# The DMAs of the output-weight sums, pinned to their place in the source's order

## The chip, the cores and the metric

The kernel runs on one core of one Trainium2 chip. The metric is device time in microseconds (us). The engines are called PE (TensorE, matrix products), DVE (VectorE), ACT (ScalarE), POOL (GpSimd) and SP (SyncE, which here does nothing but issue DMAs). Each engine works through its own list of instructions strictly in order; an instruction that waits for a semaphore holds up everything behind it on that engine.

## What is computed

The reference is one layer of a streaming encoder on 528 positions (512 inputs and 16 learned ones) of width 2048, batch 1:

```
u = rms_norm(h);  proj = u @ w_in              # 11600 columns: all inputs of both branches
A: score = sum_h w[t,h] * relu(iq[t,h] . ik[s]);  top 128 keys per query
   attention of 8 heads over these keys in a 256-wide latent space, with a bias by distance
B: softmax(q1 k1 + bias) - lam * softmax(q2 k2 + bias), 8 heads, chunk-causal; norm per head
mix = sigmoid(g_a) * ((o_a * silu(z_a)) @ w_o_a) + sigmoid(g_b) * ((o_b * silu(z_b)) @ w_o_b)
return h + rms_norm(mix @ w_out)               # w_out: 2048 x 2048
```

## The kernel before

Every product is computed with its operands split into a high and a low part, three matmuls in place of one (`mm3`, lines 288 to 291). The stages follow one another:

- **The first columns and the normalised input**, to about 90 us.
- **The index stage**, 90 to 250 us. The 16 index heads come in eight tiles of two. Tiles 2 to 7 each take two weight tiles of 512 KB ("halves"): SP loads one into `raw` (line 152), ACT makes its high part (156), DVE its low part (158), PE multiplies (289 to 291). Then PE makes the scores of the two heads (549, 550), ACT takes the relu (570), and DVE adds them up in `sc` (575).
- **Branch B**, eight heads, 230 to about 660 us. A head projects three *units* (`qb`, `kb`, `vb`). Per unit SP loads two halves of weights (187); ACT finds each half's sum of squares (`squares`, 123); POOL takes the largest over the partitions (128); DVE makes a power-of-two scale (`power_of_two`, 135 to 140); ACT and DVE split (169, 170); PE multiplies 48 or 96 times. The attention of a head runs between the products of the next one. Raw weights have room for three units, split weights for two. DVE also does the top-k search here (620, 624), a few rounds per half unit.
- **Branch A** (eight heads), the gates, the two branch projections, and from 1440 us **the output product**. This one is computed in Strassen's way: seven products in place of eight, on sums of the quarters of `w_out`. Those sums are what this case is about.

`wt_chain(k, n, tags)` makes four sums of quarters for one 128 x 512 piece, with DMAs alone: it loads two pieces (264, 265), adds another piece of DRAM to each in flight (263, a DMA issued by POOL that accumulates), stores both (260, by SP), and then twice more adds to the second tile and stores it. So one chain is load, add, put, add, put, add, put, each waiting for the one before. There are 16 chains, 32 loads, 64 adds and 64 puts, each of 256 KB; all write to DRAM (`tscr`), and the first reader of it is the output product. In the source a head of branch B starts two chains, and each of the six calls of `between()` in that head takes every chain one step on; the last step falls into the next head's first call. Chains of even and odd heads use different tiles.

The order in which instructions stand on an engine is not the source's. A scheduler of the framework puts each instruction at the place at which, by its own reckoning, it can first start; what has no operand from the computation, such as loads of weights, moves far ahead. `tc.keep_in_program_order(ins)` gives it one more edge: `ins` is queued behind the instruction that the source issued last on the same engine. It is an order of issue alone, with no wait for that instruction to finish. An instruction without such an edge may still move ahead of pinned ones.

Of the kernel before, what the change touches and what calls it, by code (L numbers as in the profile page):

```python
# [16 lines left out]
ALU = mybir.AluOpType  # L17
# [51 lines left out]
def layer_kernel(ctx, tc, xt_d, xn_d, cols_d, w0_d, wi_d, wkv_d, wo_d, wout_d, lam_d, post_d,  # L69
                 oh_d, rb_d, out_d):  # L70
    nc = tc.nc
# [8 lines left out]
    tscr = [nc.dram_tensor(f"wout_t{i + 1}", [8, P, 1024], F32, kind="Internal").ap() for i in range(4)]  # L80
# [173 lines left out]
    def wt_chain(k, n, tags):  # L254

        t = [opool.tile(HB, F32, tag=tag, name="wt") for tag in tags]
        q = [[wout_d[ci, di, k, :, 512 * n:512 * n + 512] for di in range(2)] for ci in range(2)]

        def put(i, x):
            nc.sync.dma_start(tscr[i][k, :, 512 * n:512 * n + 512], x)  # L260

        def add(x, src):
            nc.gpsimd.dma_start(x, src, accum_op=ALU.add)
        nc.sync.dma_start(t[0], q[0][0])
        nc.sync.dma_start(t[1], q[0][1])
        yield
        add(t[0], q[0][1])
        add(t[1], q[1][1])
        yield
        put(0, t[0])  # L270
        put(2, t[1])
        yield
        add(t[1], q[0][0])
        yield
        put(1, t[1])
        yield
        add(t[1], q[1][0])
        yield
        put(3, t[1])
# [488 lines left out]
    def qstack(acc, un, h):  # L768

        q = stack64(acc, un, ap_, "q", 4)  # L770
        for m in range(2):
            hs = slice(64 * m, 64 * m + 64)
            nc.scalar.activation(QZ[h % 2][m][hs], acc[hs], AF.Copy, scale=un[hs])
        return list(q) + QZ[h % 2]
# [107 lines left out]
    for h in range(NH):  # L882
        for i in range(2):
            wt_now.append(wt_chain(h, i, [f"o{6 + 4 * (h % 2) + 2 * i + x}" for x in range(2)]))
        for acc, un in proj_q("qb", h):
            step(2 if len(pending) == 7 else 1)
            between()
        q = qstack(acc, un, h)
        for acc, un in proj_kv("kb", h):
            step()  # L890
            between()
        kk = kstack(acc, un)
        if h == NH - 1:
            small_weights(0)
        for acc, un in proj_kv("vb", h):
            step()
            between()
        vt = ap_.tile([P, T], F32, tag="vt", name="vt", bufs=1)
        for t in range(2):
            nc.scalar.activation(vt[:, t * TH:(t + 1) * TH], acc[t][:, :TH], AF.Copy, scale=un)  # L900
        step(len(pending))
        pending = b_attend(h, q, kk, vt)
# [259 lines left out]
    for i in list(range(NDIRECT, NH, 2)) + list(range(NH, 2 * NH, 2)):  # L1162
        def end(x, d, i=i):
            gate_o(i + x, d.o[x], d.r[x])
        n, c0 = ("za", i) if i < NH else ("zb", i - NH)
# [335 lines left out]
```

## Time and profile before

| | |
|---|---|
| time, median of 3 (range) | 1601.42 us (1599.41 to 1604.9) |
| profiled execution | 1604.09 us, its span 1602.1 us |
| busy share of the span | PE 90%, DVE 69%, ACT 61%, POOL 9% |
| TensorE clock granted, mean | 0.961 of full speed |
| moved by DMA | 257.27 MB, 161 GB/s on average |

The profile is one execution. Busy shares are averages over stages; an idle engine is shown with the time that it sat idle and with what ended the wait. Durations of single instructions, the landing times of DMAs and the share of time in which the core's 16 DMA engines were busy come from the same execution.

### The profile page before, as it was taken

The page shows a single profiled execution, that of the slowest core. Times are in us where ns is not written, and L with a number is a line of the kernel's source. Part 1 is how long each engine was busy: PE and PEld are TensorE (multiplying, and loading weights), DVE is VectorE, ACT ScalarE, POOL GpSimd, SP SyncE. Part 2 cuts the span into 40 slices and gives each one's busy share as a digit, 9 for nine tenths or more (in the row PEclk, how much of TensorE's full clock was granted, in tenths as well). Part 3 has the DMA queues.
Part 4 walks back from the last instruction along what each step waited for, and adds up shares of the span by engine and source line. Part 5 has one row for each costly group of instructions (what it writes and reads, how often), then busy time and mean ns, then how long its engine had stood idle before and what let it go on. Part 6 is the DMA issues. An engine that isn't in the chain of part 4 may idle for free. (4 is left out here: it accounts for less than half of the span.)

```text
span 1602.1 us, 25286 instructions
## 1 busy us (share of the span) xinstructions
PE 1435.1 (90%) x9475; PEld 1076.2 (67%) x9475; DVE 1103.8 (69%) x2091; ACT 977.2 (61%) x1735; POOL 144.8 (9%) x199
## 2 busy tenths in 40 slices
PE   7895665689999999999999999999999899999997
PEld 7674443467666776656658888888888544448885
DVE  7963244376677766777567888877778555666788
ACT  6352243376666666777668778777777644436555
POOL 3512324100000000000000000000000011100001
PEclk9898777799999999999999999999999999999999
DMA  6499999932333323333264544444444544547674
GB/s 208 144 303 271 253 262 263 252 93 83 97 100 88 97 81 87 113 120 99 67 198 157 185 160 141 149 140 132 132 133 145 197 149 155 155 124 260 227 248 155
DMA packets 104218, 257.27 MB, mean 161 GB/s; under 512 B 12072, under 2 KB 16392, under 8 KB 103968
## 3 DMA queue, kind: packets, MB, share of 16 engines
q1 hardware_dynamic: 86224, 223.86, 43.4%
q0 software_dynamic: 9216, 16.78, 6.1%
q10 hardware_dynamic: 8656, 15.02, 2.6%
q8 instruction: 74, 1.21, 0.3%
q14 instruction: 48, 0.39, 0.1%
HBM read 211.42 MB, written 47.41 MB: 162 GB/s over the span
## 5 line engine op out<-in xcount | busy, mean ns | idle before, releaser
L123 ACT ACTIVATE junk<-raw 128x1024 bf16<-128x1024 f32 x192 | 201.9, 1052 | 168.0 <-DMA raw<-in_wi_dram 147.5
L289 PE MATMUL acc<-u,hi 128*128 128x264 f16 (+1 forms) x832 | 266.5, 320 | 17.5 <-ACT hi L169 16.8
L1015 PEld LDWEIGHTS <-wh 128*128 128x128 f16 x2464 | 241.6, 98 | 59.9 <-issue 31.4
L291 PE MATMUL acc<-u,lo 128*128 128x264 f16 (+1 forms) x832 | 266.1, 320 | 1.0 <-DVE lo L170 1.0
L290 PE MATMUL acc<-u,hi 128*128 128x264 f16 (+1 forms) x832 | 266.3, 320 | 0.0
L1015 PE MATMUL acc<-tu,wh 128*128 128x256 f16 x1408 | 235.6, 274 | 26.9 <-DVE r L1024 16.3
L169 ACT ACTIVATE hi<-raw,scale 128x1024 f16<-128x1024 f32 x104 | 118.9, 1145 | 131.4 <-PE acc L290 130.2
L1015 PE MATMUL acc<-tu,wl 128*128 128x256 f16 x704 | 192.7, 274 | 0.0
L1015 PE MATMUL acc<-u,wh 128*128 128x256 f16 x1056 | 175.3, 273 | 0.0
L289 PEld LDWEIGHTS <-hi 128*128 128x128 f16 x1088 | 107.6, 99 | 97.2 <-ACT hi L169 17.1
L170 DVE SCALAR_TENSOR_TENSOR lo<-raw,scale,hi 128x1024 f16<-128x1024 f32 x104 | 132.7, 1279 | 56.7 <-ACT hi L169 56.5
L291 PEld LDWEIGHTS <-lo 128*128 128x128 f16 x1088 | 107.5, 99 | 78.1 <-DVE lo L170 1.5
L290 PEld LDWEIGHTS <-hi 128*128 128x128 f16 x1088 | 107.6, 99 | 73.1 <-issue 1.2
L170 DVE SCALAR_TENSOR_TENSOR wl<-S,scale,wh 128x1024 f16<-128x1024 f32 x88 | 112.8, 1282 | 55.9 <-ACT wh L169 55.8
L1015 PE MATMUL acc<-u,wl 128*128 128x256 f16 x528 | 143.9, 273 | 0.0
L128 POOL PARTITION_ALL_REDUCE rows<-ssq x90 | 43.9, 488 | 1085.8 <-ACT junk L123 1029.3
L1015 PEld LDWEIGHTS <-wl 128*128 128x128 f16 x1232 | 120.8, 98 | 14.4
L169 ACT ACTIVATE wh<-S,scale 128x1024 f16<-128x1024 f32 x88 | 100.3, 1141 | 30.1 <-DVE S L1126 30.1
L158 DVE TENSOR_TENSOR lo<-raw,hi 128x1024 fp32r<-128x1024 f32 x40 | 48.8, 1223 | 73.9 <-ACT hi L156 73.5
L289 PE MATMUL acc<-og,hi 128*128 128x512 f16 x256 | 97.0, 379 | 0.0
L291 PE MATMUL acc<-og,lo 128*128 128x512 f16 x256 | 97.0, 379 | 0.0
L290 PE MATMUL acc<-og,hi 128*128 128x512 f16 x256 | 97.0, 379 | 0.0
(313 smaller groups left out, 2944.3 us busy)
## 6 DMA issues: line engine op xcount, KB each, us to landing
raw<-in_wi_dram SPq DMA_DIRECT2D x172, 512.0 KB, 4.9
wt<-in_wout_dram POOLq DMA_DIRECT2D x64, 256.0 KB, 7.6
wout_t<-wt SPq DMA_DIRECT2D x64, 256.0 KB, 5.9
raw<-in_wo_dram SPq DMA_DIRECT2D x32, 512.0 KB, 6.0
raw<-wout_t SPq DMA_DIRECT2D x32, 512.0 KB, 3.8
raw<-in_wout_dram SPq DMA_DIRECT2D x24, 512.0 KB, 3.6
wt<-in_wout_dram SPq DMA_DIRECT2D x32, 256.0 KB, 4.8
sg<-r ACTq DMA_DIRECT2D x32, 256.0 KB, 2.7
```

What stands on the lines that cost most here:

```text
L123: nc.scalar.activation(j, src, AF.Square, accum_out=dst)
L128: nc.gpsimd.partition_all_reduce(r, ssq, P, bass_isa.ReduceOp.max)
L158: nc.vector.tensor_sub(lo, raw, f32(hi))
L169: nc.scalar.activation(hi, src, AF.Copy, scale=s)
L170: nc.vector.scalar_tensor_tensor(lo, src, s, hi, op0=ALU.mult, op1=ALU.subtract)
L289: nc.tensor.matmul(out, aH, bH, start=start, stop=False)
L290: nc.tensor.matmul(out, aH, bL, start=False, stop=False)
L291: nc.tensor.matmul(out, aL, bH, start=False, stop=stop)
L1015: nc.tensor.matmul(acc, a[:, k, :], b, start=first and k == 0 and x == 0, stop=last and x == 2, skip_group_check=True)
```

## The change

The loads, the adds and the puts of `wt_chain` get the edge of `keep_in_program_order`. Nothing is added or removed: the same DMAs with the same operands.

```diff
         def put(i, x):
-            nc.sync.dma_start(tscr[i][k, :, 512 * n:512 * n + 512], x)
+            tc.keep_in_program_order(nc.sync.dma_start(tscr[i][k, :, 512 * n:512 * n + 512], x))

         def add(x, src):
-            nc.gpsimd.dma_start(x, src, accum_op=ALU.add)
-        nc.sync.dma_start(t[0], q[0][0])
-        nc.sync.dma_start(t[1], q[0][1])
+            tc.keep_in_program_order(nc.gpsimd.dma_start(x, src, accum_op=ALU.add))
+        for i in range(2):
+            tc.keep_in_program_order(nc.sync.dma_start(t[i], q[0][i]))
         yield
```

What this does to the lists, first on SP in the second half of the index stage. `raw_1528` and `raw_1530` are the two halves of the first unit of branch B; `wt` are tiles of the chains, with four numbers per head. Before:

```order
L260 DMA wout_t1<-wt_2855 128x512
L187 DMA raw_1528<-in_wi_dram 128x1024
L260 DMA wout_t4<-wt_2324 128x512
L260 DMA wout_t4<-wt_2328 128x512
L260 DMA wout_t3<-wt_2856 128x512
L260 DMA wout_t2<-wt_2852 128x512
L264 DMA wt_3382<-in_wout_dram 128x512
L265 DMA wt_3383<-in_wout_dram 128x512
L264 DMA wt_3386<-in_wout_dram 128x512
L187 DMA raw_1530<-in_wi_dram 128x1024
L260 DMA wout_t2<-wt_2856 128x512
L260 DMA wout_t4<-wt_2852 128x512
```

and now:

```order
L152 DMA raw_1407<-in_wi_dram 128x1024
L152 DMA raw_1467<-in_wi_dram 128x1024
L187 DMA raw_1528<-in_wi_dram 128x1024
L187 DMA raw_1530<-in_wi_dram 128x1024
L187 DMA raw_1539<-in_wi_dram 128x1024
L187 DMA raw_1541<-in_wi_dram 128x1024
L152 DMA raw_1570<-in_wi_dram 128x1024
L187 DMA raw_1798<-in_wi_dram 128x1024
L187 DMA raw_1845<-in_wi_dram 128x1024
L187 DMA raw_1847<-in_wi_dram 128x1024
L265 DMA wt_1873<-in_wout_dram 128x512
L265 DMA wt_1874<-in_wout_dram 128x512
```

All chain DMAs have left the index stage; the first chain (`wt_1873`) starts behind the loads of the first units of branch B. Next, SP in a head of branch B, with one put pair and the next head's loads; before, only the rows of lines 187, 656, 749 and 756 stood here:

```order
L656 DMA G_3832<-bias_rows 128x528
L187 DMA raw_3322<-in_wi_dram 128x1024
L187 DMA raw_3324<-in_wi_dram 128x1024
L260 DMA wout_t4<-wt_2852 128x512
L260 DMA wout_t4<-wt_2856 128x512
L265 DMA wt_3382<-in_wout_dram 128x512
L265 DMA wt_3383<-in_wout_dram 128x512
L265 DMA wt_3386<-in_wout_dram 128x512
L265 DMA wt_3387<-in_wout_dram 128x512
L187 DMA raw_3467<-in_wi_dram 128x1024
L749 DMA o9_f32<-ob_3283 128x512
L187 DMA raw_3469<-in_wi_dram 128x1024
```

Eight puts and four loads now stand between the six loads of raw weights of a head. Last, POOL in the first two heads; a `rows` is the largest sum of squares of one unit. Before:

```order
L128 ISA rows_2339<-ssq_2112 128x2
L128 ISA rows_2492<-ssq_2262 128x2
L263 DMA wt_5496<-in_wout_dram 128x512
L263 DMA wt_5500<-in_wout_dram 128x512
L128 ISA rows_2689<-ssq_2409 128x2
L128 ISA rows_2869<-ssq_2597 128x2
L128 ISA rows_3022<-ssq_2790 128x2
```

and now:

```order
L128 ISA rows_2339<-ssq_2112 128x2
L128 ISA rows_2492<-ssq_2262 128x2
L263 DMA wt_2323<-in_wout_dram 128x512
L263 DMA wt_2324<-in_wout_dram 128x512
L263 DMA wt_2327<-in_wout_dram 128x512
L263 DMA wt_2328<-in_wout_dram 128x512
L263 DMA wt_2324<-in_wout_dram 128x512
L263 DMA wt_2328<-in_wout_dram 128x512
L128 ISA rows_2689<-ssq_2409 128x2
L263 DMA wt_2324<-in_wout_dram 128x512
L128 ISA rows_2869<-ssq_2597 128x2
L263 DMA wt_2328<-in_wout_dram 128x512
```

Here six adds, which wait for loads and puts of their chain, stand ahead of the maximum `rows_2689`; from the next head on a round of eight adds lies between three maxima.

## Rows read from the trace of the kernel before

**Rows 1.** Stretches: length, busy us (instructions) per engine, clock, DMA share, GB/s.
```profile
120.00:140.00 20.00, 20.00 (x97) 16.26 (x96) 12.36 (x19) 8.70 (x19) 4.92 (x6) 1.00 1.04 305
140.00:160.00 20.00, 1.83 (x11) 1.31 (x9) 0.00 (x0) 0.00 (x0) 6.45 (x8) 0.62 1.00 238
160.00:180.00 20.00, 8.60 (x33) 6.93 (x33) 3.19 (x5) 4.78 (x10) 6.09 (x7) 0.70 0.95 250
...
300.00:320.00 20.00, 10.43 (x43) 5.77 (x44) 5.69 (x15) 7.75 (x14) 2.11 (x3) 0.61 0.83 238
sum 180.00, PE 101.03 PEld 72.89 DVE 62.72 ACT 57.40 POOL 51.75; mean PE 11.23 PEld 8.10 DVE 6.97 ACT 6.38 POOL 5.75
```
**Rows 2.** Timeline of PE: start, length, line; the wait before it and who ended it.
```profile
168.45 0.59 PE L549 MATMUL lg<-ikh,q 128*128 128x264 f32 x1 [26.61 <-ACT relu L570]
...
205.94 0.59 PE L549 MATMUL lg<-ikh,q 128*128 128x264 f32 x1 [8.80 <-ACT relu L570]
...
221.87 0.79 PE L289 MATMUL acc<-xh,hi 128*128 128x512 f32 x1 [7.76 <-ACT hi L156]
...
276.19 0.40 PE L289 MATMUL acc<-u,hi 128*128 128x264 f16 x1 [16.80 <-ACT hi L169]
...
310.05 0.90 PE L716 MATMUL acc<-ident,vt 128*128 128x128 f32 x3 [7.53 <-ACT vt L900]
```
**Rows 3.** Timeline of SP's queue, 155 to 171 us.
```profile
155.30 3.72 SPq L260 DMA_DIRECT2D wout_t<-wt  x4
159.11 1.11 SPq L187 DMA_DIRECT2D raw<-in_wi_dram  x1
...
170.93 0.38 SPq L187 DMA_DIRECT2D raw<-in_wi_dram  x1
```
**Rows 4.** Timeline of ACT, the load's first reader.
```profile
165.84 1.06 ACT L123 ACTIVATE junk<-raw 128x1024 bf16<-128x1024 f32 x1 [29.16 <-DMA raw<-in_wi_dram]
```
**Rows 5.** Timeline of POOL, a maximum behind adds.
```profile
193.10 0.37 POOL L128 PARTITION_ALL_REDUCE rows<-ssq  x1 [6.95 <-DMA wt<-in_wout_dram]
```
**Rows 6.** One whole head of branch B, columns as in rows 1.
```profile
399.60:442.20 42.60, 40.42 (x296) 29.97 (x295) 29.91 (x84) 28.33 (x56) 1.06 (x3) 1.00 0.31 94
```
**Rows 7.** Line 263's durations (ns); then landings of lines 263, 260, 265, 187.
```profile
L263 POOL DMA_DIRECT2D wt<-in_wout_dram x64: 853/862/2252, 78.8 to 309.6; - x64
...
DMA to landing us min/median/max: 3.9/7.6/12.8
...
DMA to landing us min/median/max: 2.0/5.9/8.2
...
DMA to landing us min/median/max: 3.1/6.0/6.7
...
DMA to landing us min/median/max: 3.7/4.5/9.1
```
**Rows 8.** DMA queues: packets, MB, packet time as share of 16 engines' span.
```profile
q1 hardware_dynamic: 86224, 223.86, 43.4%
q0 software_dynamic: 9216, 16.78, 6.1%
```
**Rows 9.** Timelines of SP, ACT, POOL, DVE and ACT in a head.
```profile
414.90 3.19 SPq L187 DMA_DIRECT2D raw<-in_wi_dram  x2
...
421.70 1.06 ACT L123 ACTIVATE junk<-raw 128x1024 bf16<-128x1024 f32 x1 [1.91 <-DMA raw<-in_wi_dram]
...
422.94 0.35 POOL L128 PARTITION_ALL_REDUCE rows<-ssq  x1 [15.50 <-ACT junk L123]
...
423.33 0.15 DVE L135 TENSOR_REDUCE exp<-rows 128x1 f32<-128x2 f32 x1 [5.60 <-POOL rows L128]
...
424.73 1.15 ACT L169 ACTIVATE hi<-raw,scale 128x1024 f16<-128x1024 f32 x1
```
**Rows 10.** Waits by pair, 330 to 660 us; then SP's queue, whole run: us, times, longest.
```profile
ACT hi L169 <- PE acc L290: 33.2, 15, 4.1
...
SPq L187 <- DVE lo L170: 204.2, 41, 15.4
```

## The prediction

> **What bounds the kernel now.** I read the busy time in stretches of 20 us first, from the start. The reader is to see a stage that falls out of the pattern: from 120 to 140 us PE is busy for all of the stretch, and a whole head of branch B keeps it busy for 40.42 of 42.6 us, so PE sets the pace there [rows 1, 6]; but in the nine stretches from 140 to 320 us it works 101.0 of 180 us, and its clock is granted at 0.61 to 0.70 in five of them [rows 1]. In the same stretches the DMA engines are busy for 0.83 to 1.0 and more of the time, against 0.31 in a head later on [rows 1, 6]. So some 79 us of PE's time are lost in the second half of the index stage and in head 0.
>
> Next I read who ended PE's waits there. Eight waits make up the 79 us; the largest are 26.61, 8.80, 7.76, 16.80 and 7.53 us, each ended by an ACT instruction [rows 2]. ACT itself waited: before 165.84 us it stood 29.16 us idle, at the sum of squares of a half that had not landed [rows 4]. In SP's queue that half was issued at 159.11, behind four puts that began at 155.30, and the next half only at 170.93, behind four more [rows 3]. The puts wait for adds. So the chain is: add still under way, put blocks SP, raw weights are issued late, ACT stands at the late half, relu and split stand behind it, PE stands. The weights need no such wait by themselves. POOL shows the same once more: the maximum at 193.10 had waited 6.95 us behind an add for a load of a chain [rows 5].
>
> **What the change takes away.** By the order of SP all 160 chain DMAs leave the index stage, and the loads of the first units stand together, ahead of the first chain. First term: the 79.0 us of idle PE. Second term, the clock: 33 matmuls took 8.60 us at a clock of 0.70, 97 took 20.00 us at full clock, so 33 would take 6.8: 1.8 us lost [rows 1]. Five stretches have such a clock, the others little or no loss; I take 8 us in all, between 0 and busy time times missing clock over the nine stretches, 17. Together 87 us.
>
> **What stays of it.** The last half of the index weights takes the place of the first unit's first half, so its load waits for that split; before, such a load cost PE the wait of 7.76 us [rows 2]. An undisturbed load lands 3.7 us after issue, not 8 [rows 7], so about 4 us stay. A similar wait at the start of branch B (third unit, whose second half is loaded into space that only the end of the index stage frees) gets 4 us. Bounds 0 and 15; I take 8.
>
> **What the change adds: the chains in branch B.** Work first. The 64 adds moved 16.78 MB in 6.1% of 16 engines' span, 98 us; other DMAs took 43.4% for 223.86 MB, 3.1 us per MB, so the 25.2 MB of chain loads and puts 78 us [rows 8]. Per head that is 22 us on top of 0.31 x 42.6 = 13 [rows 6]: a share of 0.83, below 1. Bandwidth alone does not stop a head.
>
> Then the waits. One round of a head's chains is a load, three adds and two puts, each waiting for the one before; the put that ends it stands on SP ahead of the next head's loads. By shortest landings that is 3.1 + 3 x 3.9 + 2 x 2.0 = 18.8 us, by medians 6.0 + 3 x 7.6 + 2 x 5.9 = 40.6, by the longest 6.7 + 3 x 12.8 + 2 x 8.2 = 61.5 [rows 7]; four adds in a row at 0.86 and four DMAs on SP make about 4 us more. The medians are those of a stage at a DMA share of 1. A head at 0.83 lies three quarters of the way from 0.31 to 1.0, so I go three quarters of the way from shortest to median: load 5.3, add 6.7, put 4.9, a round of 5.3 + 20.1 + 9.8 + 4 = 39 us. A head lasts 42.6 [rows 6]. The round fits, with 3 us to spare.
>
> Who is queued behind these waits? On SP, the raw loads. In a head a load is issued when DVE has split the old contents (SP waits for that, 41 times in the run [rows 10]), lands 4 us later, and then sum of squares, maximum and scale follow at once: 421.70, 422.94, 423.33; the next split on ACT begins at 424.73, behind them [rows 9]. What makes room in that is the split itself: ACT starts it as soon as PE frees a buffer, and waits for PE 15 times [rows 10], while PE needs it a unit later, 14.2 us (a third of a head). Both halves take 2.3 us on ACT, so some 11 us of delay cost nothing. On POOL, the maxima: in a steady head one of three stands behind three adds, the first two of which need a put landed and the third two more links. From the first add of the round: four adds issued and landed 10.2, put 4.9, two adds 8.4, put 5.2, one add 0.9: 30 us, against two units, 28.4. It comes 1 to 2 us late, inside the 11. So a steady head pays nothing as long as the round fits. I take 2 us over heads 2 to 7; bounds 0 and, if each pays 4, 24.
>
> The start is worse. In head 1 six adds stand between the maxima `rows_2492` and `rows_2689`, and in DVE's list the scale from the second one stands ahead of the low part of an earlier unit, which PE needs. From the first add of head 0 to there: 10.2 + 4.9 + 8.4 + 4.9 + 8.4, put and loads 6.6, then 10.2 + 4.9 + 1.7 + 0.4 = 61 us. In that time PE has the rest of `kb` of head 0, then `vb`, `qb`, `kb` at 11.1 us each and part of an attention, about 47. PE waits 14 us; with the shortest landings the way is 41 us and it waits 0, with medians about 20. I take 10, since the DMA engines have not yet reached 0.83 there.
>
> **Sum.** 79 + 8 - 8 - 2 - 10 = 67 us of the profiled execution's 1604.1, so 1537. That execution lay 2.7 us above the median of 1601.4, which gives 1534.
>
> **A rule that speaks against it.** An add holds POOL for 0.86 us in the median, but one took 2.25 [rows 7]; DVE was busy for 62.7 of 180 us beside them, and is for 29.9 of 42.6 in a head [rows 1, 6]. If DVE's work is what makes an add slow to issue, adds in branch B take longer: 1.4 us more each, for seven adds in the round 10 us, a round of 49 and 6 us more per head: 1534 + 7 x 6 = 1576. The Trainium skill, page "SBUF — State Buffer", section "SBUF: two separate sides", has such a rule: while DVE runs certain instructions that take both ports, GpSimd cannot write the descriptors of its DMAs. The trace hardly bears that out here: the median is 9 ns above the minimum. This rival gets 0.05.
>
> **Rivals.**
> - *The heads take on the wait* (0.18). At median landings the round is 45 us, over 42.6; with late raw loads 46 is near. For it: SP, a list in order, now carries waits for adds between raw loads, the same pattern that stopped PE before. Against it: landings outside the crowded stage are shorter. 7 x 3.4 = 24 us: 1558.
> - *The waits are gone without a price* (0.12). Shortest landings: the hitch in head 1 and the rest vanish, 87 us less: 1514; with shorter waits before 140 us, down to 1508.
> - *The index stage meets another limit* (0.05). If room for raw weights, not SP's order, holds the loads (rows 10 show that wait in its longest form, 15.4 us), PE waits as before: 1601. Against it: from 120 to 140 us loads came in time and PE was full.
> - *Slower* (0.07). Adds in branch B land as late as the longest seen, 12.8: a round of 45 + 3 x 5.2 = 61, PE waits 18 us in each of seven heads, 126 in place of the 2: 1658. It decides from a round of about 52 us on, where seven heads lose the 67 us. Against it: DMA share 0.83.
>
> **Numbers.** The forecast has 0.53 and a range of its own from 1518 to 1552. All cases: 1508 with everything gone; at the other end own waits 15, start 20 and 24 for the heads leave 87 - 59 = 28, so 1573, and the rule's 1576 is near. Range 1508 to 1576; what lies outside is the slower case and no change. About 5 us (0.3%) is what a measurement of this kernel can tell from nothing: faster 0.53 + 0.18 + 0.12 + 0.05 = 0.88, same 0.05, slower 0.07.
>
> **What would show it.** In the profile after: PE busy over 18 of 20 us in stretches from 140 us to the end of the index stage, which comes at about 195 and not 250; a DMA share near 0.3 there and near 0.8 in branch B; no wait of ACT over 10 us for raw weights in the index stage; one wait of PE of 5 to 15 us in head 1, behind `rows_2689`; stores of head results 42 to 44 us apart. I am wrong if these lie 46 us or more apart, or if PE still waits over 20 us in the index stage.

## The result and the profile after

The changed kernel took 1554.01 us in the median of its runs (1552.04 to 1558.84), the kernel before 1603.16 beside it (1599.41 to 1606.07): a ratio of 0.970, with a 95% interval of 0.967 to 0.973. The forecast was 1534 with a range of 1508 to 1576. So the direction and the range held, and 20 us of the forecast gain did not come. The main case's own range, 1518 to 1552, was missed by 2 us.

The stretches of the profile after, with the columns of [rows 1]: length, busy us (instructions) of PE, PEld, DVE, ACT and POOL, clock, DMA share, GB/s. The fifth row is one head, from one store of a head result to the next, and answers to [rows 6].

```profile
140.00:160.00 20.00, 19.87 (x94) 15.82 (x93) 11.34 (x20) 10.09 (x22) 0.38 (x1) 1.00 0.26 79
160.00:180.00 20.00, 19.92 (x98) 14.87 (x97) 12.74 (x21) 13.49 (x26) 3.96 (x12) 1.00 0.32 88
180.00:200.00 20.00, 20.00 (x131) 13.63 (x130) 18.70 (x56) 12.89 (x27) 3.09 (x6) 1.00 0.64 208
...
220.00:240.00 20.00, 12.23 (x60) 6.94 (x59) 5.83 (x17) 8.23 (x14) 4.64 (x7) 0.83 0.86 237
372.07:421.82 49.75, 43.11 (x296) 31.91 (x295) 32.17 (x90) 28.43 (x56) 8.68 (x12) 0.90 0.74 188
```

From 140 to 200 us PE is full at full clock, where before it worked 1.83 of 20 us at worst. That loss is gone, and the last scores of the index stage come at 188.2 us and not at 243.1. But the head lasts 49.75 us and not 42.60, with the same 296 matmuls.

The stores of head results date the rest. These are four of them in SP's queue (start, length, line), the first, the third, the fourth and the seventh:

```profile
281.79 0.96 SPq L749 DMA_DIRECT2D o_f<-ob  x1
...
372.07 0.33 SPq L749 DMA_DIRECT2D o_f<-ob  x1
421.82 0.33 SPq L749 DMA_DIRECT2D o_f<-ob  x1
...
566.29 0.32 SPq L749 DMA_DIRECT2D o_f<-ob  x1
```

Before, the first was issued at 357.16 and the seventh at 617.16. So 75.4 us are gained up to the first store. The six heads after it take 284.5 us in place of 260.0 (47.4 each in place of 43.3; the head shown is the second longest of them) and give 24.5 back, and what follows gives back another 3: 48 us of span, from 1602.1 to 1554.1.

How much of the 24.5 us is idle time, and how much a lower clock? The six heads, before and now:

```profile
357.16:617.16 260.00, 245.72 (x1767) 181.72 (x1766) 183.75 (x500) 169.52 (x331) 6.38 (x18) 0.99 0.31 92
```
```profile
281.79:566.29 284.50, 254.00 (x1766) 188.56 (x1765) 185.70 (x501) 170.10 (x331) 44.49 (x62) 0.94 0.74 192
```

For the same matmuls PE is busy 8.3 us longer, at a granted clock of 0.94 in place of 0.99, and idle for 16.2 us more.

Who waits in these six heads? Waits by pair (us in all, times, longest) of ACT, PE and DVE, before (357 to 617 us) and now (282 to 567 us):

```profile
ACT junk L123 <- DMA raw<-in_wi_dram: 31.7, 25, 4.3
...
PE acc L675 <- DVE pr L744: 11.0, 6, 2.2
...
DVE kl L785 <- ACT kh L784: 2.5, 6, 0.4
```

```profile
ACT junk L123 <- DMA raw<-in_wi_dram: 63.5, 24, 5.7
...
PE acc L675 <- DVE pr L744: 28.8, 6, 6.6
...
DVE kl L785 <- ACT kh L784: 41.3, 6, 7.5
DVE z L742 <- ACT p L668: 27.9, 8, 4.7
DVE exp L135 <- POOL rows L128: 7.8, 14, 1.6
```

PE has one long wait in each head, at the transposes of the softmax result `pr`. The chain behind it can be read in one head, on SP, ACT, DVE and PE:

```profile
371.51 0.33 SPq L187 DMA_DIRECT2D raw<-in_wi_dram  x1
...
373.80 0.33 SPq L187 DMA_DIRECT2D raw<-in_wi_dram  x1
...
379.44 1.06 ACT L123 ACTIVATE junk<-raw 128x1024 bf16<-128x1024 f32 x1 [4.77 <-DMA raw<-in_wi_dram]
...
380.49 0.51 ACT L668 ACTIVATE pr<-pr,mx 128x272 f32<-128x272 f32 x1
...
383.69 1.06 ACT L123 ACTIVATE junk<-raw 128x1024 bf16<-128x1024 f32 x1 [2.09 <-DMA raw<-in_wi_dram]
...
395.44 1.06 ACT L123 ACTIVATE junk<-raw 128x1024 bf16<-128x1024 f32 x1 [1.39 <-DMA raw<-in_wi_dram]
...
398.89 1.06 ACT L123 ACTIVATE junk<-raw 128x1024 bf16<-128x1024 f32 x1 [2.30 <-DMA raw<-in_wi_dram]
...
400.07 0.47 ACT L784 ACTIVATE kh<-acc,scale 64x264 fp32r<-64x264 f32 x1
...
381.63 0.16 DVE L742 RECIPROCAL z<-z 128x1 f32<-128x1 f32 x1 [4.08 <-ACT p L668]
...
400.58 0.48 DVE L785 SCALAR_TENSOR_TENSOR kl<-acc,scale,kh 64x264 fp32r<-64x264 f32 x1 [6.62 <-ACT kh L784]
...
408.90 1.94 PE L675 MATMUL acc<-ident,pr 128*128 128x128 f32 x8 [6.58 <-DVE pr L744]
```

The halves issued at 371.51 and 373.80 are first read at 379.44 and 383.69, 8 and 10 us later; in [rows 9] the second half, issued at about 418, was read at 421.70, 4 us later. ACT works through its list in order. Its sum of squares (line 123) stands idle for the half, the exponentials of the softmax (line 668) stand right behind it in the list, and DVE waits 4.08 us for them; PE still has work then. The same thing happens with the next two halves, and now it reaches PE. Their sums of squares stand idle at 395.44 and 398.89, and right behind them, at 400.07, stands `kh` (line 784), the copy of the keys whose product PE had finished at about 396. DVE waits 6.62 us for it, with the next softmax behind it, and PE 6.58 us for that. The clock then adds to the wait. Stretches of the same head:

```profile
392.00:402.00 10.00, 10.00 (x91) 8.79 (x89) 3.00 (x7) 5.02 (x9) 1.94 (x3) 1.00 0.58 163
402.00:412.00 10.00, 3.42 (x18) 2.65 (x17) 9.60 (x24) 5.72 (x11) 0.04 (x1) 0.62 0.72 164
412.00:421.82 9.82, 9.82 (x70) 8.43 (x69) 6.03 (x19) 6.85 (x13) 3.90 (x5) 0.86 0.80 236
```

After the idle time the granted clock is 0.62 and then 0.86. Over the head PE is busy 43.11 us in place of 40.42, so 2.7 us of its loss are clock and the rest idle time.

### The profile page after: what moved, and what is told of

The parts are those of the page before. It is cut to its first block, busy times and chain, and to the rows that moved or that the text cites. A ratio compares the mean times of both kernels' runs of the same rounds, so it can differ in the third digit from the quotient of the medians.

```text
span 1554.1 us, 25269 instructions
## 1 busy us (share of the span) xinstructions
PE 1438.2 (93%) x9475; PEld 1079.5 (69%) x9475; DVE 1104.7 (71%) x2091; ACT 978.3 (63%) x1735; POOL 144.3 (9%) x199
## 5 line engine op out<-in xcount | busy, mean ns | idle before, releaser
L128 POOL PARTITION_ALL_REDUCE rows<-ssq x90 | 47.4, 527 | 1066.9 <-ACT junk L123 960.5
L170 DVE SCALAR_TENSOR_TENSOR wl<-raw,scale,wh 128x1024 f16<-128x1024 f32 x66 | 84.3, 1278 | 10.0 <-ACT wh L169 9.9
```

The costliest lines, as they stand in the source:

```text
L128: nc.gpsimd.partition_all_reduce(r, ssq, P, bass_isa.ReduceOp.max)
L170: nc.vector.scalar_tensor_tensor(lo, src, s, hi, op0=ALU.mult, op1=ALU.subtract)
```

## The experiments

Three theories for the 24.5 us were set against each other. A: the chains' transfers share the DMA engines with the raw halves, which land late. B: SP's order holds the raw loads behind waiting puts. C: POOL's maxima stand behind adds. A fourth, D, stands in the first expectation alone: DVE and ACT stand in another order. Times are compared as ratios to the kernel before, on the same chip; 0.01 is 16 us. "First" and "heads" are the first store and the mean of the six heads after it.

| kernel | median us | ratio (95%) | first, us | heads, us |
|---|---|---|---|---|
| before | 1597 to 1603 | 1 | 357.2 | 43.3 |
| after | 1554.0 | 0.970 (0.967-0.973) | 281.8 | 47.4 |
| no chains | 1503.4 | 0.941 (0.939-0.942) | 259.3 | 42.7 |
| traffic without links | 1548.4 | 0.970 (0.968-0.971) | 272.6 | 47.7 |
| late puts | 1553.4 | 0.973 (0.970-0.976) | 273.6 | 48.6 |
| chains spread | 1579.9 | 0.989 (0.987-0.990) | 277.2 | 52.5 |
| half adds | 1533.6 | 0.961 (0.959-0.963) | 271.3 | 46.1 |
| loads alone pinned | 1605.2 | 1.005 (1.004-1.007) | 309.2 | 51.5 |
| two heads' chains in the index stage | 1555.6 | 0.975 (0.973-0.978) | 286.9 | 46.3 |
| after + squares pinned | 1509.1 | 0.946 (0.944-0.948) | 269.6 | 42.3 |
| no chains + squares pinned | 1479.5 | 0.926 (0.923-0.929) | 254.1 | 41.0 |
| before + squares pinned | 1585.1 | 0.992 (0.989-0.995) | 358.3 | 41.0 |
| after + squares pinned, bias early | 1500.6 | 0.939 (0.936-0.942) | 267.3 | 41.6 |

**No chains.**

```diff
-            wt_now.append(wt_chain(h, i, ...))
+            pass
```

> Left out: all chain DMAs; the output product reads plain quarters of the weights in place of the four sums, so the result is not the reference's. Theory A (shared DMA engines): adds, puts and loads of the chains make raw weights land late in the heads of branch B, and ACT, which reads them in order, holds up the softmax. Theory B (SP's order): raw loads are issued late because SP stands at puts that wait for adds. Theory C (POOL's order): maxima stand behind adds. All three: without chains the heads go back from 47.7 us apart to 43.5, as before the change, the start of branch B loses part of its waits of 18 us, and the time falls from 1554 to 1515 to 1525. Theory D, the heads are longer because DVE and ACT stand in another order: 1545 to 1554.

It took 1503, below the expected range: the heads came to 42.7, and more went at the start than was counted on. In the kernel after the chains therefore cost 0.029, some 47 us; in the profiled executions it is 4.7 us in each of six heads, 22.5 before the first store, and 4 behind the heads. D alone, 1545 to 1554, is out.

**The same traffic without links**: puts store a tile that nothing writes, adds go to tiles that were written long before. One of the changed lines:

```diff
-        put(1, t[1])
+        put(1, free[2])
```

> The same number of loads, adds and puts with the same bytes, pinned at the same places, but without links: puts store a tile that nothing writes, adds go to tiles whose last writer is long done. The sums that the output product reads are wrong. Theory A: bytes and places are the same, so heads stay 46 to 48 us apart, raw loads land as late as with the change, 1545 to 1555. Theory B and C: no wait is left on SP or ahead of the maxima, heads 43.5 us, 1518 to 1530.

The time is within what A expected. Nothing is gained in the heads, 47.7 us each. ACT's and PE's waits from 272 to 559 us are those of the kernel after; the last row is POOL's:

```profile
ACT junk L123 <- DMA raw<-in_wi_dram: 63.6, 26, 5.3
...
PE acc L675 <- DVE pr L744: 29.1, 6, 6.1
```
```profile
POOL rows L128 <- ACT junk L123: 171.1, 18, 17.6
```

Only the first store came earlier, by 9 us. In a steady head the loss is that of the transfers themselves, without their links. This speaks against B: SP waits at no put for an add here (33.6 us in the kernel after), and a group of four puts takes 2.4 us on it, not 8.60. It speaks against C as well. POOL's adds still waited for earlier adds, but all 18 maxima of the six heads waited for a sum of squares on ACT, none for an add. DVE's waits are others, though: 51.0 us for these maxima, against 7.8 in the kernel after, and 2.5 for `kh`. The late sum of squares reaches DVE by the maximum here, and by `kh` there.

**Late puts, and chains spread.** Each put one half unit later (one of three places is shown); then, in a kernel of its own, the chains begun one every three half units and not in pairs.

```diff
         yield
+        yield
         put(0, t[0])
```

> Every put one half unit later than its add (ten steps per chain in place of seven), the same work and result. Theory B: the adds have landed when SP comes to the put, SP no longer stands, heads 43.5 to 45 us, 1525 to 1537. Theory A: the same bytes per head, within 5 us of 1554. Theory C: adds on POOL wait less for puts or as long, within 5 us.

> The 16 chains start one every three half units in place of two every six, so that bursts of four loads, adds or puts become bursts of two. Same work and result. Theory A: shorter bursts, raw loads land 1 to 3 us earlier, heads 45 to 46.5 us, 1540 to 1549. Theory B: as many waits of SP for adds, only at other places, 1550 to 1558. Theory C: never more than two adds of one step ahead of a maximum, 1545 to 1552.

Late puts change nothing that can be told. But they do not test B: SP waited 37.1 us at puts for adds in the six heads, where it had waited 33.6, so the wait that was to go did not go. What speaks against B in the kernel after is the kernel without links. The spread chains missed what all three theories expected: slower, heads of 52.5 us. SP's queue shows why, and ACT the cost:

```profile
382.76 18.23 SPq L260 DMA_DIRECT2D wout_t<-wt  x6
...
402.69 0.86 SPq L187 DMA_DIRECT2D raw<-in_wi_dram  x2
...
409.55 1.06 ACT L123 ACTIVATE junk<-raw 128x1024 bf16<-128x1024 f32 x1 [11.06 <-DMA raw<-in_wi_dram]
```

Six puts came to stand in a row, 18 us long, and the raw loads behind them, though DVE's splits, which make room for them, were done by 398.4. So B is a real mechanism when the row of puts is long: in the kernel after a group of four took 8.60 us on SP, here six took 18.23.

**Half adds.**

```diff
-... nc.gpsimd.dma_start(x, src, accum_op=ALU.add)
+... nc.gpsimd.dma_start(x[:, :256], src[:, :256], accum_op=ALU.add)
```

> The 64 accumulating transfers on POOL's queue move half of the columns (8.4 MB in place of 16.8 MB), so the sums are incomplete; loads, puts, links and the order of every engine are those of the kernel after. Theory A (the raw halves land late in branch B because the adds' bytes share the DMA engines with them): half of the adds' bytes gives back about half of what the adds cost, the six steady heads come to some 45 us each (270 in place of 284.5), and the time to 1535-1545. If the number of linked transfers counts and not their bytes (issue, latency, order): 1550-1556, heads still 47 apart. If the chain round of a head decides: shorter landings would shorten it, 1530-1540, with SP's puts waiting less.

1533.6, just below A's 1535 to 1545; the heads came to 46.1, 1.3 us less, not 2.4. The time alone fits the third expectation better, that the chain's round decides (1530 to 1540), and SP's wait at puts did fall, from 33.6 to 16.9 us in the six heads; but the kernel without links had no such wait and no faster heads. ACT's wait for raw halves fell with the bytes:

```profile
ACT junk L123 <- DMA raw<-in_wi_dram: 46.4, 24, 3.5
```

**One part of the change alone**: only the loads pinned, the edit here against the kernel before.

```diff
-        nc.sync.dma_start(t[0], q[0][0])
-        nc.sync.dma_start(t[1], q[0][1])
+        for i in range(2):
+            tc.keep_in_program_order(nc.sync.dma_start(t[i], q[0][i]))
```

> One part of the change alone: the loads of the chains keep the source's place, puts and adds are left to the scheduler. If the loads alone carry the change (no load, so nothing to add or put in the index stage): puts and adds can only come later than their loads, PE is full in the index stage as after, and the time is within 1545-1565. If the scheduler draws the adds and puts together into crowds (as six puts stood in a row on SP in the kernel with the chains spread): 1570-1600.

The whole gain is gone, and the time lies above even the second expectation, 1570 to 1600, though the chains have left the index stage. A head with chains and one after the last of them:

```profile
309.19:374.71 65.52, 45.56 (x296) 32.58 (x294) 30.22 (x92) 28.82 (x57) 14.96 (x19) 0.81 0.88 221
...
489.30:531.79 42.49, 40.42 (x296) 29.93 (x295) 31.84 (x86) 28.33 (x56) 1.06 (x3) 1.00 0.31 94
```

Adds and puts went as early as their data allowed, 19 POOL instructions a head in place of 12. First and last add of line 263 (ns min/median/max, first and last start in us), here and in the kernel after:

```profile
L263 POOL DMA_DIRECT2D wt<-in_wout_dram x64: 856/866/1852, 180.7 to 444.9; - x64
```
```profile
L263 POOL DMA_DIRECT2D wt<-in_wout_dram x64: 861/902/1897, 197.3 to 545.3; - x64
```

The same 64 adds lie in 264 us here, in 348 in the kernel after, and in 231 before [rows 7]. SP's own wait from 309 to 442 us, for two heads of this kernel:

```profile
SPq L260 <- DMA wt<-in_wout_dram: 100.1, 32, 9.1
```

SP stood at puts for 100 of 133 us, with raw loads between them: the pattern of the kernel before, in another stage. Leaving the index stage is thus not enough; without the pins on adds and puts there is no gain. These pins set a pace, one link per half unit, and a place among the raw loads; which of the two does it was not separated.

**The chains of two heads in the index stage**, where the DMA engines had a share of 0.26 to 0.32.

```diff
+                if j in (2, 5) and at == 0:
+                    wt_pair(j // 3)
...
-            wt_now.append(wt_chain(h, i, ...))
+        if 1 <= h < NH - 1:
+            wt_pair(h + 1)
```

> The chains of two of the eight heads are begun in the index stage (at its third and sixth pair of units), where PE was full and the DMA share 0.26-0.32; the first head and the last have none; all else as after. Theory A (a head with chains costs about 4.5 us by shared DMA engines, plus the start): two heads and the start without them give back 8-20 us if the index stage takes them at no price: 1535-1546. If puts in SP's order stop the index stage's loads (as in the kernel before): PE waits there again for ACT, 10-20 us, and the time is 1550-1565.

No gain, and the time and the wait are those of the second expectation. The wait of the kernel before is back in small. SP, ACT and a PE wait, then one stretch of the index stage (lines 553 and 574 of this kernel are 549 and 570 of the kernel before):

```profile
136.40 4.17 SPq L260 DMA_DIRECT2D wout_t<-wt  x4
...
152.30 1.06 ACT L123 ACTIVATE junk<-raw 128x1024 bf16<-128x1024 f32 x1 [18.63 <-DMA raw<-in_wi_dram]
```
```profile
PE lg L553 <- ACT relu L574: 16.1, 1, 16.1
```
```profile
140.00:160.00 20.00, 5.10 (x15) 4.28 (x16) 3.19 (x5) 4.25 (x8) 1.72 (x2) 0.57 0.64 177
```

**The squares pinned**: the sums of squares on ACT keep the source's place, with all transfers of the kernel after.

```diff
-            squares(self.raw[hf], self.ssq[:, hf:hf + 1])
+            tc.keep_in_program_order(squares(self.raw[hf], self.ssq[:, hf:hf + 1]))
```

> The sums of squares of the halves on ACT keep their place in the source's order, so that they do not stand ahead of the softmax exponentials and of the other work that PE asks for; all transfers as in the kernel after. If the loss in a head is ACT standing at a late half with the softmax behind it (the 5.7 us waits), the waits of DVE for `p` and of PE for `pr` in the steady heads go, heads come to 43-45.5 us and the time to 1525-1540. If the place of the sums of squares does not matter (the units themselves come too late, whatever stands behind them): 1550-1558. If the maxima on POOL become just in time behind the adds (theory C): slower than the kernel after, 1560-1580, with DVE waiting for rows of POOL.

1509.1 us: 0.024 less, some 39 us, and heads of 42.3, both below what was expected (1525 to 1540, 43 to 45.5). One head (396.03 to 436.10), with more DMA work than in the head shown of after, and PE's waits in the six heads:

```profile
396.03:436.10 40.07, 39.41 (x291) 29.48 (x290) 30.32 (x76) 26.88 (x54) 8.21 (x11) 1.00 0.86 227
```
```profile
PE acc L675 <- DVE pr L744: 5.2, 6, 3.2
PE acc L675 <- DVE PL L688: 2.9, 4, 1.8
```

The raw halves land no earlier: in the six heads 4.0/5.4/7.2 us after issue (min/median/max) against 3.7/4.7/8.9 in the kernel after. But no wait of ACT for them is left, against 63.5 us. SP stands 135.9 us at puts in these heads, and PE's waits there are still short. The pin also moved POOL's maxima ahead of adds in the list. That is not where the gain lies, as far as the rows tell: DVE waited 7.8 us for maxima in the kernel after and 10.9 here, and the kernel without links lost as much in its heads with no maximum behind an add.

Two controls tell how much of this is the pin's own: the same edit on the kernel without chains (the first, against the kernel after), and on the kernel before (the second, against that kernel).

```diff
-            wt_now.append(wt_chain(h, i, ...))
+            pass
-            squares(self.raw[hf], ...)
+            tc.keep_in_program_order(squares(self.raw[hf], ...))
```

> No chain DMAs at all (the output product reads quarters that were not summed), and the sums of squares pinned on ACT as in the kernel that took 1509. If the pin only lets the heads bear late halves, there is nothing to bear here, and the time is that of the kernel without chains and without the pin, 1497-1509, heads 42.5 us apart. If the pinned order of ACT is the better one in any case: 1465-1490, heads 39-41 us apart; the chains then still cost 20-40 us in the kernel with the pin.

```diff
-            squares(self.raw[hf], ...)
+            tc.keep_in_program_order(squares(self.raw[hf], ...))
```

> The kernel before with one part more and none of the change: the chains' DMAs left to the scheduler, the sums of squares pinned on ACT. If in the index stage too the loss came from ACT standing at late halves with other work behind it: 1530-1560. If the halves come too late in themselves there, since SP stands at crowded puts while raw loads wait behind them: 1580-1605, PE still at 5-15 of 20 us between 160 and 320 us.

Without chains the pin is worth 0.015, some 24 us, so the first expectation failed and the second held: the order of ACT is the better one in any case. In the kernel without chains and without the pin, too, ACT had stood for raw halves, 30.1 us in six heads, at a landing of 3.7 us in the median. Beyond that the pin bears the late halves. A head pays 4.7 us for chains without the pin (42.7 to 47.4) and 1.3 with it (41.0 to 42.3). In the whole run the chains still cost 0.020, some 32 us, with the pin, against 47 without it; 15.5 of them lie before the first store. On the kernel before the pin is worth 0.008, 13 us, as the second expectation had it: its heads come to 41.0, but the first store comes no earlier (358.3). One stretch of its index stage and a wait of DVE:

```profile
200.00:220.00 20.00, 0.00 (x0) 0.00 (x0) 0.00 (x0) 0.00 (x0) 5.40 (x7) 0.50 1.04 256
```
```profile
226.49 0.15 DVE L135 TENSOR_REDUCE exp<-rows 128x1 f32<-128x2 f32 x1 [40.20 <-POOL rows L128]
```

DVE waits once 40.2 us for a maximum on POOL, with relu and PE behind it; POOL's adds stand ahead of that maximum. This is C, at its full price, in a kernel where the adds are not pinned.

**Bias tile early.** In the kernel with pinned squares PE waited 6.72 us in head 1. SP, DVE and PE:

```profile
251.74 2.04 SPq L260 DMA_DIRECT2D wout_t<-wt  x2
253.87 0.38 SPq L656 DMA_DIRECT2D G<-bias_rows  x1
...
257.25 0.11 DVE L657 MEMSET G<- 64x64 f32 x1 [8.44 <-DMA G<-bias_rows]
...
260.04 0.69 PE L675 MATMUL acc<-ident,pr 128*128 128x128 f32 x2 [6.72 <-DVE PL L688]
```

```diff
     for h in range(NH):
+        g = bias_tile(NH + h)        # its load pinned on SP
```

> The kernel with the pinned sums of squares (1509), and the load of a head's bias tile G put at the head's start, pinned on SP, where it stood behind a put that waited for an add (DVE waited 8.4 us for it in head 1, 1.4 to 7 in others). If these waits were on the path of PE: 8-12 us less, 1496-1502, first store of a head result at 260. If the next late thing takes their place (PE then waits for a softmax or a split): 1504-1510.

1500.6 us (0.939), within what was expected, and the fastest kernel that does the whole work. Yet the place is not as expected: the first store moved by 2.3 us only, and DVE waited longer for G, 35.6 us in place of 15.4 from 80 to 640 us. The wait of 6.72 us is gone; other waits took most of it, and the rest of the 10 us of span came in small parts, 3.9 in the six heads and 3.8 behind them. What gave these was not settled.

## Why the prediction was right, and where it was off

**The index stage: right.** The mechanism read from [rows 2 to 4] went as the sum said: PE at 19.87, 19.92 and 20.00 of 20 us to the end of the stage, a DMA share of 0.26 to 0.32 there, and no ACT wait over 4.1 us from 100 to 200 us. The waits of the start were forecast at 8 + 10 us; in the kernel after PE's waits from 205 to 275 us come to 17.9. They are five of 1.1 to 4.5 us, though, and not one behind `rows_2689`. Up to the first store the terms make 79 + 8 - 8 - 10 = 69 us, against 75.4. But the reason was half of it: the kernel with loads alone pinned shows that chains taken out of the index stage cost as much elsewhere, when their adds and puts are left to the scheduler.

**The heads: the step that failed.** The sum had "2 us over heads 2 to 7"; measured were 24.5, at the upper bound of 24 and at the price of the rival "the heads take on the wait", whose 1558 lies nearer to the measured 1554 than the forecast's 1534. By the prediction's own sign of being wrong, stores 46 us or more apart, this part failed: they lie 47.4 apart. The rival had the number and not the mechanism, since it went by waits for adds on SP, and the kernel without links has none of them. The range held because it had this price in it. The step behind the 2 us was "Both halves take 2.3 us on ACT, so some 11 us of delay cost nothing". It looked at who waits for the split, and found slack. For the index stage the prediction had read the right thing, ACT at a late half with relu and split behind it; for the heads it did not ask the same. There it did not look at what stands behind the late half's first reader in ACT's own list: the sum of squares, placed early by the scheduler, with the copy of the keys and the softmax of the running head behind it. The prediction's own rows had that idle ACT, 1.91 us at 421.70 [rows 9], and it was not priced. With the sums of squares pinned, the chains' price in a head fell from 4.7 to 1.3 us; what makes the 1.3 was not settled. The round of the chain fitted in the head, as worked out; the loss needs no overrun (traffic without links costs the same), and no fuller DMA engines than thought: their share in the head is 0.74, forecast was 0.83.

**The clock: a term left out of the heads.** The prediction gave back 8 us of clock in the index stage, but charged none to new waits. In the six heads 8.3 of the 24.5 us are busy time at the lower clock, in the head shown 2.7 of some 7.

**The rule that speaks against it** did not decide: an add held POOL for 902 ns in the median and 1897 at most, against 862 and 2252 [rows 7]. The Trainium skill, page "SBUF — State Buffer", section "SBUF: two separate sides", has DVE keep GpSimd from writing descriptors while DVE runs certain instructions; a median 40 ns longer is all that this trace could give to it.

**The rival on the slower side** (adds as late as the longest seen) did not come: landings were 3.7/5.4/12.5 us, shorter than the 3.9/7.6/12.8 of before [rows 7], and the median under the 6.7 that the sum took.

## What to carry to other kernels

When a transfer becomes late, ask what stands behind its first reader in that engine's list, not only who needs its result: an early, unimportant instruction that waits for data holds up everything that follows. Taking background transfers out of a crowded stage is not enough by itself: their links take their waits along, and here the gain came only when each link was given its place. An experiment that is meant to take a wait away says something only if the wait went: late puts left SP's wait as it was, and told nothing of it. Try a cheap pin on the first reader together with the pin on the transfers; here the second was worth 0.030 of the time and the first another 0.024.

## What the runs showed of the hardware

A raw half of 512 KB landed in 3.6/3.7/5.1 us (min/median/max, six heads) without chains, and in 3.7/4.7/8.9 beside adds and puts at a DMA share of 0.74: the slow end moved far more than the median. And at a share of 0.86 (the head with pinned squares) PE still ran 39.41 of 40.07 us, so a high share by itself stopped nothing.
